# One step by seven products fewer in every second early block, and another order of the opening work

## The chip, the cores and the metric

The kernel runs on one core of one Trainium2 chip. Its time is device time in microseconds (us). Three runs of the kernel before took 1721.94, 1722.01 and 1723.89; the median is 1722.01. All times below are in us unless marked ns.

A core has a matrix engine (TensorE; PE in the profile, with its weight loads as PEld), an elementwise engine (VectorE; DVE), an engine for activation functions and copies with scale (ScalarE; ACT), GpSimd (POOL) and a queue engine (SyncE; SP) that here only starts transfers. Each engine works through its own instructions in the order in which they were written, and waits for the others by semaphores.

## What is computed

The reference is one layer of a decoder on 256 positions of width 2048, all in float32. Cut to what matters here:

```python
a = rmsnorm(h, norm_mix_pre)
proj = a @ w_in                        # 256 x 2048 times 2048 x 17408
q_a, k_a, v_a, q_r, f_r, i_r, g_r, gate_a, gate_r = split_columns(proj)
# three groups of sliding-window attention with rotary q and k
qh, kh = rotary(heads(q_a)), rotary(heads(k_a))
# a gated linear recurrence; its lower bound comes from hgrn_lower_bounds
f = lb + (1.0 - lb) * sigmoid(f_r)
r_out = norm(recurrence(silu(q_r), log(f), 1 - f, i_r)) * hgrn_norm_gain * silu(g_r)
y = sigmoid(gate_a) * (attn @ w_attn_branch) + sigmoid(gate_r) * (r_out @ w_hgrn_branch)
h = h + rmsnorm(y @ w_mix_out, norm_mix_post)
a = rmsnorm(h, norm_ffn_pre)
h = h + rmsnorm((silu(a @ W_gate) * (a @ W_up)) @ w_ffn_down, norm_ffn_post)
```

Here `lb` is the first entry of a softmax over the two rows of `hgrn_lower_bounds`. The first norm's factor per row is not multiplied into `a`; it is called `r1c` and is applied where the products leave the accumulators.

## The kernel before

Each float32 factor is split into a high and a low part (`hi` by a copy on ScalarE, `lo` by a subtraction on VectorE), and each product is made from three matmuls: high by high, high by low, low by high. The weights stream through SBUF: SP loads a `raw` tile, the two engines split it, TensorE multiplies.

**Blocks and steps.** The whole program is one list of steps, `seq` (main loop from L1351 on). A block is a set of output columns; a step is the part of a block with one slice of the contracted rows. In turn n the loop first issues the split of step n + 2 and the load for the unit three behind that one (`ahead`, `load_behind`), then the matmuls of step n, and then it advances some Python generators by one `yield` each: the evacuation of the block before (`evacs`), and two lanes of side work (`lanes[0]`, `lanes[1]`). So a `yield` in such a generator moves what follows it one step later, on every engine. The order on each engine is the order of this loop.

The list begins with two blocks for the gate `g_r` (halves 0 and 1, 8 steps each, 12 matmuls of 512 columns a step; steps 0 to 15). Then come the eight early blocks of the kind `Wide` (steps 16 to 79), each 1024 columns by 8 steps: four branch gates, three times the values `v`, and `i`. Behind them come the blocks with rotary, the recurrence, attention, the output projections and the feed-forward part.

**Steps by seven products.** In a `Wide` block a step covers two row groups (one pair `m`) and two column groups, so it is a 2 x 2 by 2 x 2 block product. A plain step makes it from eight products (24 matmuls of 512 columns). A step marked 1 in the block's order makes it from seven (21 matmuls), in the manner of Strassen and Winograd: `split_wide` (L319 to L349) first forms sums of weight quarters (`sum`, L333, L339, L340), splits these into `hi` (L338, L341) and `lo` (`wl`, L346), and splits three of the quarters themselves into `dh` (ScalarE, L344) and `dl` (VectorE, L348). A plain step needs one `hi` (L327) and one `lo` (`wl`, L329). On the other side a step by seven needs sums of the activations of its pair, `x7[m]`, which `pair_sums` (L415) makes in lane 1: a first part on VectorE (`f`, `s`; L420, L405 to L409), one copy on ScalarE (`so`, L411), one subtraction on VectorE (`so`, L413), each a step apart. The first nine of the 21 matmuls read `dh` and `dl`; the last twelve do not.

Two orders are used in the early blocks: `EIGHT` has steps by seven at the indices 2, 4 and 6 (pairs 0, 1, 2), `FOUR` at 1, 3, 5 and 6 (pairs 0, 1, 2, 3). Blocks 0, 2, 4 and 6 take `EIGHT`, blocks 1, 3, 5 and 7 take `FOUR`. The odd blocks exchange the roles of the two pools of accumulator banks (`flip`). Of `hi` there are three slots in turn, of `wl` three, of `sum` one, of `dh` and `dl` two each in the early blocks and one each in the feed-forward blocks, whose order is `EIGHT` too. When the last step by seven of a block is done, `gather` (L389) takes its four partial sums out of the banks, and the block's evacuation follows behind the last step.

**The opening.** `opening` (L580) runs in lane 0 from step 0: sums of squares, four transfers on ScalarE's queue (among them `rowg`, the rows with the norm gain and the lower bounds, and `cs`, cosines and sines); at step 8 the norm's factor `r1c`; then `row_broadcast` (L512), which writes `diag` on VectorE, multiplies it with ones on TensorE one step later and copies the result to `rowb` on ScalarE another step later; then the rotary tables `tabs` (L597); then a transpose of `rowg` on TensorE (L604), and from that the bounds `lb` and `lb1` (L606 to L617) with two Exp on ScalarE.

**The gate halves.** `evac_g` (L737) waits until `r1c` is announced in `ready`, then issues four activations from the accumulators (Sigmoid and Copy, L744, L745), yields once, and then issues per side two products on VectorE (L748, L749) and a store on POOL's queue, a side a step. For half 1 this runs during block 0. In a `Wide` block the evacuations still open are finished at once when the step with index `turn` is done; `turn` is 1 in the early blocks.

Of the kernel before, what the change touches and what calls it, by code (L numbers as in the profile page):

```python
# [14 lines left out]
F32R = mybir.dt.float32r  # L15
I32 = mybir.dt.int32
AF = mybir.ActivationFunctionType
OP = mybir.AluOpType
# [10 lines left out]
QSCALE = HD ** -0.5  # L29
# [3 lines left out]
COL_QR, COL_FR, COL_IR, COL_GR = 9216, 10240, 11264, 12288  # L33
COL_GA, COL_GB = 13312, 15360

X7, H7 = (0, 1, 2, 3), (0, 1, 2)
FOUR = [(4, 0), (0, 1), (5, 0), (1, 1), (6, 0), (2, 1), (3, 1), (7, 0)]
EIGHT = [(3, 0), (4, 0), (0, 1), (5, 0), (1, 1), (6, 0), (2, 1), (7, 0)]
DOWN = [[(m, m in by7) for m in range(KF // 2)] for by7 in (range(4, 20, 3), range(3, 19, 3))]

N_RAW, N_SPLIT, AHEAD, WARM, BRIDGE = 3, 3, 2, 8, 6


class Block:
# [46 lines left out]
def tile_hybrid_block(ctx: ExitStack, tc: tile.TileContext, t, out):  # L91
    nc = tc.nc
# [13 lines left out]
    def nm(s):  # L106
        serial[0] += 1
        return f"{s}_{serial[0]}"
# [7 lines left out]
    def aux():  # L116
        return auxp.tile([P, 512], F32, tag="aux", name=nm("aux"))
# [4 lines left out]
    def p3(s, dtype, n, bufs, tag=None):  # L122
        return pool["now"].tile([P, n], dtype, tag=tag or s, bufs=bufs, name=nm(s))
# [4 lines left out]
    def small(s, n=8, bufs=6):  # L128
        return cpool.tile([P, n], F32, tag=f"small{n}", bufs=bufs, name=nm(s))

    def mm(ps, lhsT, rhs, start, stop):
        nc.tensor.matmul(ps, lhsT, rhs, start=start, stop=stop, skip_group_check=True)  # L132
# [35 lines left out]
    r1c = cpool.tile([P, 2], F32, name="r1c")  # L168
# [3 lines left out]
    rowb = cpool.tile([P, S], F32, name="rowb")  # L172

    stage = ctx.enter_context(ExitStack())
    pool = {}
# [23 lines left out]
    cs = kp.tile([P, 2, S], F32, name="cs")  # L199
    gainr = kp.tile([P, HW], F32, name="gainr")  # L200
    tabs = kp.tile([P, 4, S], F32, name="tabs")
# [16 lines left out]
    def add_seven(*args, flip, **kw):  # L218
        b = Wide(*args, **kw)
        b.flip = flip  # L220
        blocks.append(b)
        for i in range(b.steps):
            seq.append(Step(b, i, len(units), 0))
            units.append([seq[-1]])
# [53 lines left out]
    def wslot():  # L278
        return stream.tile([P, 2048], F32R, tag="w", bufs=N_SPLIT, name=nm("w"))
# [39 lines left out]
    def split_wide(st):  # L319

        b, raw = st.block, st.raw
        m, by7 = b.order[st.i]
        prep = b.prep(m, by7) if b.prep else iter(())
        next(prep, None)
        hi, lo = wslot(), p3("wl", F32R, 2048, 3)
        if not by7:
            nc.scalar.activation(hi, raw, AF.Copy)  # L327
            next(prep, None)
            nc.vector.tensor_sub(lo, raw, hi.bitcast(F32))  # L329
            st.parts = hi, lo  # L330
            return
        s, d = p3("sum", F32, 2048, 1), raw[:, 512:]
        nc.vector.tensor_sub(  # L333
            s[:, :1024].rearrange("p (a c) -> p a c", a=2),
            raw[:, 512:1536].rearrange("p (a c) -> p a c", a=2),
            raw[:, None, :512].to_broadcast([P, 2, 512]),
        )
        nc.scalar.activation(hi[:, :1024], s[:, :1024], AF.Copy)  # L338
        nc.vector.tensor_add(s[:, 1024:1536], raw[:, 512:1024], s[:, 512:1024])  # L339
        nc.vector.tensor_sub(s[:, 1536:], raw[:, 1536:], s[:, 1024:1536])  # L340
        nc.scalar.activation(hi[:, 1024:], s[:, 1024:], AF.Copy)  # L341
        next(prep, None)
        dhi, dlo = (p3(x, F32R, 1536, 2 if pool["name"] == "early" else 1) for x in ("dh", "dl"))
        nc.scalar.activation(dhi, d, AF.Copy)  # L344
        for x in (slice(0, 2048),) if b.prep else (slice(0, 1024), slice(1024, 2048)):
            nc.vector.tensor_sub(lo[:, x], s[:, x], hi[:, x].bitcast(F32))  # L346
        next(prep, None)
        nc.vector.tensor_sub(dlo, d, dhi.bitcast(F32))  # L348
        st.parts = hi, lo, dhi, dlo  # L349
# [162 lines left out]
    def row_broadcast(dst, rc):  # L512

        ds = [small("diag", P, 2) for _ in range(2)]
        for b in range(2):
            nc.vector.tensor_scalar(ds[b], ident, rc[:, b : b + 1], None, op0=OP.mult)
        yield
        ps = aux()
        for b in range(2):
            mm(ps[:, b * P : (b + 1) * P], ones[:, :P], ds[b], True, True)  # L520
        yield
        nc.scalar.activation(dst, ps[:, :S], AF.Copy)
# [13 lines left out]
    ready = set()  # L536
# [24 lines left out]
    xT = Split("xT", KD)  # L561
# [18 lines left out]
    def opening():  # L580
        ss, s2 = small("ss"), small("s2")
        yield from sumsq(ss, xt[:3])
        nc.scalar.dma_start(gainr, t["hgrn_norm_gain"].to_broadcast([P, HW]))
        nc.scalar.dma_start(rowg[0:16], t["norm_ffn_pre"][0].rearrange("(a p) -> a p", p=P))
        nc.scalar.dma_start(
            rowg[16:32], t["hgrn_lower_bounds"].rearrange("l (a p) -> (l a) p", p=P)
        )
        nc.scalar.dma_start(cs, t["rope"])
        yield from sumsq(ss, xt[3:], 3)
        add_parts(s2[:, :2], ss)  # L590
        rsqrt_mean(r1c, s2[:, :2], D)
        ready.add("r1c")
        yield from row_broadcast(rowb, r1c)
        ready.add("rowb")
        yield
        for i, (j, c) in enumerate(((0, -QSCALE), (1, -QSCALE), (0, 1.0), (1, 1.0))):
            nc.vector.scalar_tensor_tensor(  # L597
                out=tabs[:, i, :].rearrange("p (two j) -> p two j", two=2),
                in0=cs[:, j, :].rearrange("p (j two) -> p two j", two=2), scalar=c,
                in1=rowb.rearrange("p (two j) -> p two j", two=2), op0=OP.mult, op1=OP.mult,  # L600
            )
        yield
        ps = aux()
        nc.tensor.transpose(ps[:, :32], rowg[:32], ident[:32, :32])  # L604
        yield
        nc.vector.tensor_copy(colg[:, 16:48], ps[:, :32])  # L606
        l0, l1 = colg[:, 32:40], colg[:, 40:48]
        m, e0, e1 = small("m"), small("e0"), small("e1")
        nc.vector.tensor_max(m, l0, l1)
        nc.vector.tensor_sub(e0, l0, m)  # L610
        nc.vector.tensor_sub(e1, l1, m)
        nc.scalar.activation(e0, e0, AF.Exp)
        nc.scalar.activation(e1, e1, AF.Exp)
        nc.vector.tensor_add(e1, e0, e1)
        nc.vector.reciprocal(e1, e1)
        nc.vector.tensor_mul(lb, e0, e1)
        nc.vector.tensor_scalar(lb1, lb, -1.0, 1.0, op0=OP.mult, op1=OP.add)  # L617
        ready.add("lb")

    def keep_warm(n):  # L620

        ps = aux()
        for _ in range(n):
            mm(ps, warm[:, :P], warm, True, True)
# [15 lines left out]
    x7 = {}  # L640
# [20 lines left out]
    def evac_kept(key, fn):  # L661
        def go(b):
            dst, at = keep(key, 1024), [(0, 0), (0, 1), (1, 0), (1, 1)]
            for k in at:
                nc.vector.tensor_add(b.rest[k], b.bank[k], b.rest[k])
            for s, g in at:
                e = b.rest[s, g]
                nc.scalar.activation(e, e, fn, scale=r1c[:, s : s + 1])
                nc.gpsimd.dma_start(dst[:, s, g * 512 : (g + 1) * 512], e)
                if (s, g) == (0, 1):  # L670
                    yield
            yield
        return go
# [63 lines left out]
    def evac_g(half):  # L737
        def go(banks):
            while "r1c" not in ready:
                yield  # L740
            dst, there = hslot("g"), keep(("g", half), 512)
            s = [ptile("sig") for _ in banks]
            for i, ps in enumerate(banks):
                nc.scalar.activation(s[i], ps, AF.Sigmoid, scale=r1c[:, i : i + 1])  # L744
                nc.scalar.activation(dst[:, i, :], ps, AF.Copy, scale=r1c[:, i : i + 1])  # L745
            yield
            for i in range(2):
                nc.vector.tensor_mul(dst[:, i, :], dst[:, i, :], s[i])  # L748
                nc.vector.tensor_mul(  # L749
                    dst[:, i, :], dst[:, i, :], gainr[:, half * 512 : (half + 1) * 512]  # L750
                )
                nc.gpsimd.dma_start(there[:, i, :], dst[:, i, :])
                yield
        return go
# [519 lines left out]
    w_in = t["w_in"][0]  # L1274
# [14 lines left out]
    for half in range(2):  # L1289
# [3 lines left out]
    early = [(COL_GA, ("a", 0), AF.Sigmoid), (COL_GB, ("r", 0), AF.Sigmoid),  # L1293
             (COL_GA + 1024, ("a", 1), AF.Sigmoid), (COL_GB + 1024, ("r", 1), AF.Sigmoid)]
    early += [(COL_V + 1024 * g, ("v", g), AF.Copy) for g in range(3)] + [(COL_IR, "i", AF.Copy)]
    for n, (col, key, fn) in enumerate(early):
        add_seven(w_in, (col, col + 512), FOUR if n % 2 else EIGHT, xT, lambda m: x7[m],
                  evac_kept(key, fn), flip=n % 2 == 1, turn=1,
                  pre=({0: lambda: advance(evacs), 1: lambda: flush(lanes[1])}).get(n))
    for half in range(2):  # L1300
        add_wide(w_in, KD, COL_FR + 512 * half, xT, evac_f(half))
# [49 lines left out]
    for n, st in enumerate(seq):  # L1351
        b, i = st.block, st.i
# [32 lines left out]
    a, b, c = seq[-3:]  # L1385
# [61 lines left out]
```

## Time and profile before

| what | value |
|---|---|
| median of three runs | 1722.01 |
| the profiled execution's own time | 1722.4 |
| its span in the trace | 1720.6 |
| granted TensorE clock, mean | 0.998 |
| TensorE (PE) busy | 1699.2 (99%) |
| VectorE (DVE) busy | 1404.6 (82%) |
| ScalarE (ACT) busy | 908.2 (53%) |
| read from HBM | 331.83 MB, 200 GB/s over the span |

A row of the timeline has the start in us from the begin of the span, the duration, engine, line, operation, the tiles written and read, the shapes and how many instructions the row merges; in square brackets stands the idle time of the engine before the row, and who ended it. A row of waits has who waited for whom, the sum in us, how often, and the longest. A row of windows has the stretch and its length, then busy time and instructions of each engine, the granted clock, the share of the DMA engines and GB/s. Durations of matmuls include their latency, and they overlap: the distance between two starts is what one costs. Some matmul records are missing from the trace, so counts of matmuls in a window can be a few too low.

### The profile page before, as it was taken

How to read it: one execution, taken by the hardware profiler on the slowest of the kernel's cores; microseconds unless marked ns; L12 is line 12 of the kernel's file. 1: busy time of each engine (PE TensorE's matmuls, PEld its weight loads, DVE VectorE, ACT ScalarE, POOL GpSimd, SP SyncE). 2: the span in 40 equal slices, each digit the busy share in tenths (PEclk: the TensorE clock that was granted, in tenths of full speed). 3: DMA queues.
4: the chain of work that ended last, by engine and by line, in shares of the span. 5: the costliest groups of instructions: out<-in, count | busy, mean ns of one | idle time of the engine just before them, and what ended most of it. 6: DMA issues, size and time to landing. Idle time of an engine off the chain costs nothing.

```text
span 1720.6 us, 21632 instructions
## 1 busy us (share of the span) xinstructions
PE 1699.2 (99%) x8334; PEld 1425.1 (83%) x8335; DVE 1404.6 (82%) x1577; ACT 908.2 (53%) x1027; POOL 40.1 (2%) x72
## 2 busy tenths in 40 slices
PE   9999999999999999999999999999999999999997
PEld 7788888878888898888888878888888888888886
DVE  6999898986677887877665578888888888898998
ACT  7556465554434434544444466555555555665663
POOL 0000000001000000000000000000000000000000
PEclk9999999999999999999999999999999999999999
DMA  8666666668544655465555745555555555666653
GB/s 279 212 216 242 211 229 219 230 211 285 173 166 164 214 163 174 160 207 172 171 171 183 258 161 206 196 199 201 202 202 201 202 201 198 207 198 216 200 197 117
DMA packets 206615, 344.79 MB, mean 200 GB/s; under 512 B 10960, under 2 KB 77568, under 8 KB 206512
## 3 DMA queue, kind: packets, MB, share of 16 engines
q1 hardware_dynamic: 198208, 317.89, 54.9%
q0 software_dynamic: 5680, 19.60, 3.3%
q10 hardware_dynamic: 2624, 5.92, 1.0%
q8 instruction: 65, 1.06, 0.2%
q14 instruction: 38, 0.31, 0.0%
HBM read 331.83 MB, written 11.53 MB: 200 GB/s over the span
## 4 chain that ended last, share of the span: by engine, by line
PE 77%; DVE 1%; ACT 1%; issue 1%; ACTq 0%; DVEq 0%
PE acc L132 52%; PE aux L132 23%; PE aux L818 0%; PE acc L1132 0%; DVE fz L1261 0%; PE aux L1132 0%; DVE dl L348 0%; PE aux L480 0%; PE aux L492 0%; ACT junk L1215 0%; ACT dh L344 0%; ACTq L1016 0%; DVE e L1211 0%; DVE sum L333 0%; ACT w L292 0%
## 5 line engine op out<-in xcount | busy, mean ns | idle before, releaser
L293 DVE TENSOR_TENSOR w<-raw,w 128x1024 fp32r<-128x1024 f32 (+1 forms) x225 | 274.1, 1219 | 189.0 <-ACT w L292 188.3
L292 ACT ACTIVATE w<-raw 128x1024 fp32r<-128x1024 f32 (+1 forms) x225 | 237.1, 1054 | 291.0 <-PE acc L132 243.1
L132 PE MATMUL acc<-xT,w 128*128 128x256 f32 (+1 forms) x2048 | 370.4, 339 | 0.0
L132 PEld LDWEIGHTS acc<-xT,w 128*128 128x128 f32 x2048 | 311.6, 188 | 43.3
L329 DVE TENSOR_TENSOR wl<-raw,w 128x2048 fp32r<-128x2048 f32 x118 | 269.9, 2289 | 76.1 <-ACT w L327 74.9
L327 ACT ACTIVATE w<-raw 128x2048 fp32r<-128x2048 f32 x118 | 225.0, 1909 | 112.0 <-PE aux L132 49.6
L132 PE MATMUL acc<-w,hT 128*128 128x512 f32 x622 | 181.5, 391 | 0.3 <-ACT hT L499 0.3
L338 ACT ACTIVATE w<-sum 128x1024 fp32r<-128x1024 f32 x70 | 74.4, 1063 | 190.2 <-DVE sum L333 181.1
L346 DVE TENSOR_TENSOR wl<-sum,w 128x1024 fp32r<-128x1024 f32 (+1 forms) x128 | 168.6, 1321 | 0.0
L132 PE MATMUL acc<-w,xT 128*128 128x512 f32 x480 | 139.3, 393 | 0.3 <-DVE w L293 0.2
L132 PEld LDWEIGHTS acc<-w,hT 128*128 128x128 f32 x622 | 116.0, 188 | 24.6 <-ACT hT L499 0.5
L132 PE MATMUL aux<-w,hT 128*128 128x512 f32 x430 | 135.6, 389 | 0.0
L348 DVE TENSOR_TENSOR dl<-raw,dh 128x1536 fp32r<-128x1536 f32 x70 | 123.0, 1757 | 8.8 <-ACT dh L344 6.7
L132 PE MATMUL aux<-w,xT 128*128 128x512 f32 x344 | 108.5, 389 | 0.0
L132 PEld LDWEIGHTS acc<-w,xT 128*128 128x128 f32 x480 | 89.2, 188 | 20.0 <-DVE w L293 1.6
L344 ACT ACTIVATE dh<-raw 128x1536 fp32r<-128x1536 f32 x70 | 103.1, 1473 | 0.0
L132 PEld LDWEIGHTS aux<-w,hT 128*128 128x128 f32 x430 | 80.7, 188 | 16.7
L132 PE MATMUL acc<-w,yT 128*128 128x512 f32 x384 | 88.2, 390 | 0.3 <-DVE w L293 0.3
L341 ACT ACTIVATE w<-sum 128x1024 fp32r<-128x1024 f32 x70 | 74.4, 1062 | 21.5 <-DVE sum L340 21.5
L333 DVE TENSOR_TENSOR sum<-raw 128x1024 f32<-128x1024 f32 x70 | 85.2, 1217 | 0.2 <-DMA raw<-in_w_ffn_down 0.2
L132 PEld LDWEIGHTS acc<-w,yT 128*128 128x128 f32 x384 | 71.8, 188 | 15.5 <-DVE w L293 0.7
L132 PE MATMUL aux<-w,a 128*128 128x512 f32 x268 | 83.7, 389 | 0.0
(261 smaller groups left out, 2737.8 us busy)
## 6 DMA issues: line engine op xcount, KB each, us to landing
raw<-in_w_in SPq DMA_DIRECT2D x271, 512.0 KB, 4.5
raw<-in_w_ffn_gate_up SPq DMA_DIRECT2D x176, 512.0 KB, 4.4
raw<-in_w_ffn_down SPq DMA_DIRECT2D x88, 512.0 KB, 4.8
raw<-in_w_mix_out SPq DMA_DIRECT2D x32, 512.0 KB, 4.9
kept<-e POOLq DMA_DIRECT2D x32, 256.0 KB, 4.4
raw<-in_w_hgrn_branch SPq DMA_DIRECT2D x16, 512.0 KB, 4.9
raw<-in_w_attn_branch SPq DMA_DIRECT2D x16, 512.0 KB, 4.5
v<-kept POOLq DMA_DIRECT2D x8, 512.0 KB, 7.3
```

Source lines behind the costliest of these rows:

```text
L132: nc.tensor.matmul(ps, lhsT, rhs, start=start, stop=stop, skip_group_check=True)
L292: nc.scalar.activation(wh[:, k], raw[:, k], AF.Copy)
L293: nc.vector.tensor_sub(wl[:, k], raw[:, k], wh[:, k].bitcast(F32))
L327: nc.scalar.activation(hi, raw, AF.Copy)
L329: nc.vector.tensor_sub(lo, raw, hi.bitcast(F32))
L333: nc.vector.tensor_sub(s[:, :1024].rearrange("p (a c) -> p a c", a=2), raw[:, 512:1536].rearrange("p (a c) -> p a c", a=2), raw[:, None, : ...
L338: nc.scalar.activation(hi[:, :1024], s[:, :1024], AF.Copy)
L341: nc.scalar.activation(hi[:, 1024:], s[:, 1024:], AF.Copy)
L344: nc.scalar.activation(dhi, d, AF.Copy)
L346: nc.vector.tensor_sub(lo[:, x], s[:, x], hi[:, x].bitcast(F32))
L348: nc.vector.tensor_sub(dlo, d, dhi.bitcast(F32))
```

## The change

All eight early blocks take the order `EIGHT`: three steps by seven, of the pairs 0, 1 and 2. The order `FOUR` and the sums of the fourth pair, `x7[3]`, are gone; `more_x` still starts the pairs 0 and 2 at step 6 and now pair 1 alone at step 7. `dh` and `dl` have one buffer each in all stages.

In `opening` the transpose of `rowg` comes directly behind the norm's factor, in the same step; the bounds follow in the next two steps; `r1c` is announced after the two Exp, one step later than before; then comes `row_broadcast`; and the rotary tables come after 16 more yields, which is in step 28, in block 1. The announcement of `rowb`, which nothing waited for, is gone.

For half 1 of the gate, `evac_g` yields four times instead of once between its activations and its products, and block 0 finishes open evacuations only at its step with index 6 instead of 1.

```diff
-X7, H7 = (0, 1, 2, 3), (0, 1, 2)
-FOUR = [(4, 0), (0, 1), (5, 0), (1, 1), (6, 0), (2, 1), (3, 1), (7, 0)]
+X7 = H7 = (0, 1, 2)
 EIGHT = [(3, 0), (4, 0), (0, 1), (5, 0), (1, 1), (6, 0), (2, 1), (7, 0)]
...
-N_RAW, N_SPLIT, AHEAD, WARM, BRIDGE = 3, 3, 2, 8, 6
+N_RAW, N_SPLIT, AHEAD, WARM, BRIDGE, LATER = 3, 3, 2, 8, 6, 16
...
-        dhi, dlo = (p3(x, F32R, 1536, 2 if pool["name"] == "early" else 1) for x in ("dh", "dl"))
+        dhi, dlo = (p3(x, F32R, 1536, 1) for x in ("dh", "dl"))
...
         rsqrt_mean(r1c, s2[:, :2], D)
-        ready.add("r1c")
-        yield from row_broadcast(rowb, r1c)
-        ready.add("rowb")
-        yield
-        for i, (j, c) in enumerate(((0, -QSCALE), (1, -QSCALE), (0, 1.0), (1, 1.0))):
-            nc.vector.scalar_tensor_tensor(
-                out=tabs[:, i, :].rearrange("p (two j) -> p two j", two=2),
-                in0=cs[:, j, :].rearrange("p (j two) -> p two j", two=2), scalar=c,
-                in1=rowb.rearrange("p (two j) -> p two j", two=2), op0=OP.mult, op1=OP.mult,
-            )
-        yield
         ps = aux()
         nc.tensor.transpose(ps[:, :32], rowg[:32], ident[:32, :32])
         yield
...
         nc.scalar.activation(e0, e0, AF.Exp)
         nc.scalar.activation(e1, e1, AF.Exp)
+        ready.add("r1c")
+        yield
         nc.vector.tensor_add(e1, e0, e1)
         nc.vector.reciprocal(e1, e1)
         nc.vector.tensor_mul(lb, e0, e1)
         nc.vector.tensor_scalar(lb1, lb, -1.0, 1.0, op0=OP.mult, op1=OP.add)
         ready.add("lb")
+        yield from row_broadcast(rowb, r1c)
+        for _ in range(LATER):
+            yield
+        for i, (j, c) in enumerate(((0, -QSCALE), (1, -QSCALE), (0, 1.0), (1, 1.0))):
+            nc.vector.scalar_tensor_tensor(
+                out=tabs[:, i, :].rearrange("p (two j) -> p two j", two=2),
+                in0=cs[:, j, :].rearrange("p (j two) -> p two j", two=2), scalar=c,
+                in1=rowb.rearrange("p (two j) -> p two j", two=2), op0=OP.mult, op1=OP.mult,
+            )
...
-            yield
+            for _ in range(1 if half == 0 else 4):
+                yield
             for i in range(2):
                 nc.vector.tensor_mul(dst[:, i, :], dst[:, i, :], s[i])
...
-        add_seven(w_in, (col, col + 512), FOUR if n % 2 else EIGHT, xT, lambda m: x7[m],
-                  evac_kept(key, fn), flip=n % 2 == 1, turn=1,
+        add_seven(w_in, (col, col + 512), EIGHT, xT, lambda m: x7[m],
+                  evac_kept(key, fn), flip=n % 2 == 1, turn=1 if n else 6,
```

## The prediction

> **What bounds the kernel now.** I read the page's busy shares first, then busy time stage by stage, then what PE waited for, then the timelines of the places where it waited. The page:
>
> ```profile
> span 1720.6 us, 21632 instructions
> ...
> PE 1699.2 (99%) x8334; PEld 1425.1 (83%) x8335; DVE 1404.6 (82%) x1577; ACT 908.2 (53%) x1027; POOL 40.1 (2%) x72
> ```
>
> TensorE is the bound; a change can gain only by fewer matmuls or by filling PE's gaps. The early blocks, one window per block (us; PE, PEld, DVE, ACT and POOL busy with counts; granted clock, DMA share, GB/s):
>
> ```profile
> 56.10:101.14 45.04, 42.34 (x184) 34.20 (x183) 43.26 (x43) 25.67 (x23) 1.08 (x2) 1.00 0.63 223
> 101.14:144.25 43.11, 41.41 (x182) 33.65 (x181) 40.61 (x36) 24.99 (x22) 2.17 (x4) 1.00 0.63 219
> 144.25:185.72 41.47, 41.47 (x185) 34.35 (x184) 36.23 (x33) 22.35 (x20) 2.16 (x4) 1.00 0.66 229
> 185.72:228.81 43.09, 41.42 (x182) 33.64 (x181) 40.60 (x36) 24.96 (x22) 2.17 (x4) 1.00 0.63 220
> ...
> 270.28:313.35 43.07, 41.40 (x182) 33.63 (x180) 40.58 (x36) 24.95 (x22) 2.17 (x4) 1.00 0.64 219
> 313.35:354.83 41.48, 41.48 (x185) 34.35 (x183) 36.25 (x33) 22.36 (x20) 2.16 (x4) 1.00 0.68 229
> 354.83:397.86 43.03, 41.38 (x181) 33.63 (x180) 39.66 (x37) 24.93 (x24) 3.11 (x6) 1.00 0.62 208
> ```
>
> Blocks 2 and 6 (and 4, left out) have three steps by seven products and PE is busy in the whole window. Blocks 1, 3, 5 and 7 have four, so 12 matmuls less than eight plain steps instead of 9, and yet they take longer, with PE idle for 1.7. Block 0 has three and takes 45.04. PE's waits between 40 and 400 us, and the longest one behind that:
>
> ```profile
> PE acc L132 <- DVE dl L348: 6.7, 8, 0.9
> PE aux L132 <- DVE dl L348: 1.3, 1, 1.3
> PE aux L132 <- DVE wl L329: 0.9, 1, 0.9
> PE aux L132 <- ACT dh L344: 0.5, 1, 0.5
> ```
>
> ```profile
> PE aux L492 <- DVE h L1065: 0.8, 1, 0.8
> ```
>
> Eight waits for dl are two in each four-step block; the other three rows are block 0. On PE's timeline:
>
> ```profile
> 57.42 0.50 PE L132 MATMUL aux<-wl,xT 128*128 128x512 f32 x1 [0.93 <-DVE wl L329]
> ...
> 68.21 0.39 PE L132 MATMUL aux<-dh,xT 128*128 128x512 f32 x1
> ...
> 72.06 0.39 PE L132 MATMUL acc<-w,so 128*128 128x512 f32 x1
> ...
> 79.05 0.50 PE L132 MATMUL aux<-dh,xT 128*128 128x512 f32 x1 [0.47 <-ACT dh L344]
> 80.84 0.50 PE L132 MATMUL aux<-dl,xT 128*128 128x512 f32 x1 [1.29 <-DVE dl L348]
> ```
>
> From 68.21 to 72.06 PE issues the first to the 18th matmul of one step: 3.85/17 = 0.2265 a matmul. So a plain step (24) takes 5.44 and one by seven (21) 4.76. The 0.39 of a row is its latency, not its price.
>
> Why VectorE is late in a four-step block: here is VectorE where its split of a step by seven begins (sum), and where a plain step's begins (wl, L329).
>
> ```profile
> 118.07 2.29 DVE L329 TENSOR_TENSOR wl<-raw,w 128x2048 fp32r<-128x2048 f32 x1
> 120.28 1.22 DVE L333 TENSOR_TENSOR sum<-raw 128x1024 f32<-128x1024 f32 x1
> ...
> 127.13 1.22 DVE L333 TENSOR_TENSOR sum<-raw 128x1024 f32<-128x1024 f32 x1
> ```
>
> A plain step costs VectorE 2.2 (118.07 to 120.28), one by seven 6.85 (120.28 to 127.13). A plain one and one by seven are 9.1 against 10.2 on PE: VectorE keeps up. Two by seven in a row, as indices 5 and 6 of the four-step order are, are 13.7 against 9.5: it falls behind. That is the second wait; the first, at index 3, comes since index 1's split lies just before the evacuation of the block before.
>
> **The change part by part.** *Three steps everywhere.* Blocks 1, 3, 5 and 7 become what 2, 4 and 6 are, with only the roles of the bank pools exchanged. I take the measured difference: 43.11, 43.09, 43.07 and 43.03 against 41.47 and 41.48 is 1.64 + 1.62 + 1.60 + 1.56 = 6.4 less. It contains 3 x 0.2265 = 0.68 for the added matmuls of each block, 2.7 in all; the vanished waits, with the restart behind each, are the other 9.1. Each converted step gives VectorE 6.85 - 2.2 = 4.6 back. [...]
>
> *One dh and one dl instead of two.* ScalarE's dh of a step may now start only when PE is through with the dh of the one by seven before. In block 2:
>
> ```profile
> 167.13 0.39 PE L132 MATMUL acc<-dh,xT 128*128 128x512 f32 x1
> ...
> 169.14 1.48 ACT L344 ACTIVATE dh<-raw 128x1536 fp32r<-128x1536 f32 x1
> ```
>
> PE's last use of the old dh ends at 167.52; the next dh, with a second buffer at hand, was written only from 169.14. The reason is structural: hi of that split comes earlier on ScalarE and needs the w slot that PE frees just before it begins the step whose dh is in question. So the added wait has ended 1.6 earlier: nothing. If that cover went, ScalarE would stand with the next hi queued behind dh.
>
> *The opening.* I number steps from 0: 0-7 and 8-15 are the two gate halves, 16-23 block 0. Rows between the norm and step 16:
>
> ```profile
> 37.36 0.16 DVE L150 SCALAR_TENSOR_TENSOR r1c<-a,y 128x2 f32<-128x2 f32 x1
> ...
> 37.90 1.28 ACT L744 ACT_TABLE_LOAD   x1
> ...
> 41.49 1.07 ACT L292 ACTIVATE w<-raw 128x1024 fp32r<-128x1024 f32 x1
> ...
> 43.74 0.69 DVE L748 TENSOR_TENSOR g<-g,sig 128x512 f32<-128x512 f32 x1
> ...
> 45.07 1.22 DVE L293 TENSOR_TENSOR w<-raw,w 128x1024 fp32r<-128x1024 f32 x1
> ...
> 47.53 1.42 DVE L597 SCALAR_TENSOR_TENSOR tabs<-cs,rowb 128x256 f32<-128x256 f32 x4
> ...
> 51.75 0.18 DVE L606 COPY colg<-aux 128x32 f32<-128x32 f32 x1
> ...
> 53.43 0.68 DVE L420 TENSOR_TENSOR f<-xT 128x512 f32<-128x512 f32 x1
> ...
> 55.09 2.28 DVE L329 TENSOR_TENSOR wl<-raw,w 128x2048 fp32r<-128x2048 f32 x1
> ```
>
> PE's first wait is for the wl that starts at 55.09 and ends at 57.37; VectorE has no long gap from 45.07 (split of step 13) to there, 12.3. Between those points the change takes away the tables (1.4) and the bounds (51.75 to 53.43, 1.7) and puts in the first pair of gate products, which comes one step later as r1c is announced one step later (43.74 to 45.07, 1.3): 10.5. But the stretch also begins later. ScalarE's two Exp now come first, behind VectorE's so, one split and four small bounds operations (37.5 + about 2.4 = 39.9); Exp to 40.2, split of 12 to 41.2, then table load and four gate evacuations (37.90 to 41.49: 3.6), so, and the split of 13 to about 46.4. Queued behind the Exp on ScalarE are those splits; PE takes up step 12 only at about 44.4 (the row of 48 matmuls below begins with step 6; 27.77 + 72 x 0.2265, and a transpose between), so that wait is hidden. 46.4 + 10.5 = 56.9 against 57.37: of the wait at 57.42 only about 0.45 goes. The ends: nothing of it goes, or all of it (0.93 by its row, some 1.2 with the restart). Two table loads of 1.28 leave ScalarE, off the path.
>
> Two new orders on PE: the transpose of rowg moves to the end of step 8, the matmuls with ones to the end of step 11. The first waits for a DMA:
>
> ```profile
> 27.77 11.14 PE L132 MATMUL acc<-w,xT 128*128 128x512 f32 x48
> ```
>
> ```profile
> L585 ACTq DMA_DIRECT2D rowg<-in_hgrn_lower_bounds x1: 442/442/442, 29.0 to 29.0; - x1
> ```
>
> ```profile
> rowg<-in_hgrn_lower_bounds ACTq DMA_DIRECT2D x1, 8.0 KB, 6.1
> ```
>
> It lands at 35.1; step 8 ends at 27.77 + 36 x 0.2265 = 35.9. Nothing, with 0.8 to spare. The ones need diag: behind the sums of an x pair (1.66 from 39.9), the split of 12, the rest of the bounds and diag itself, some 2.4 together, that is 44.0; PE is there at 44.4. The tables go to step 28, behind the split of a step by seven, where the even blocks' VectorE is idle for some us (41.47 - 36.23 = 5.2 a block): nothing.
>
> *Block 0's second wait*, at step 20 (79.05 and 80.84). Ahead of that split on VectorE lay:
>
> ```profile
> 67.33 0.69 DVE L748 TENSOR_TENSOR g<-g,sig 128x512 f32<-128x512 f32 x1
> ...
> 68.66 0.69 DVE L420 TENSOR_TENSOR f<-xT 128x512 f32<-128x512 f32 x1
> ...
> 72.52 0.68 DVE L748 TENSOR_TENSOR g<-g,sig 128x512 f32<-128x512 f32 x1
> ...
> 73.85 1.22 DVE L333 TENSOR_TENSOR sum<-raw 128x1024 f32<-128x1024 f32 x1
> ```
>
> The gate products (1.33 twice) now come behind the splits of 21 and 22, and the sums of the fourth x pair (68.66 on, 1.66) are gone: 4.3 less, with 0.45 from above, so dl stands at about 80.8 - 4.75 = 76.0. PE wants it at 78.6 - 0.45 = 78.1. The wait goes. Next at risk is dl of step 22: one product pair (1.33) is back before it, so it comes 3.4 earlier, while PE comes 2.7 earlier; there was no wait, and there is none. The gate's stores on POOL move some steps; nothing stands behind them until block 0's stores. SP's loads follow the splits that free their raw, which are earlier.
>
> Block 0: 45.04 - 41.47 = 3.57 above an undisturbed block; about 0.85 stays: 2.7 gained. **Sum: 6.4 + 2.7 = 9.1.** The profiled execution is 1722.4 (span 1720.6 and 1.8 around it), so 1713.3; it is 0.4 above the runs' median of 1722.01, so I forecast 1712.9 as a median. The block-0 term runs from 2.3 (its first wait stays whole) to 3.57 (both go), and I allow the 0.4 between profiled execution and median once downwards: 1711.6 to 1713.3.
>
> **The rivals.** *Block 0's loss stays* (its products only move to collide with step 22, or rowg is late): 1722.0 - 6.4 = 1715.6. For it: slack at 22 is thin. *One of the two waits of an odd block survives*, four times about 1.1: 1722.0 - 9.1 + 4.4 = 1717.3. Against: VectorE is less loaded than in front of block 2, which had no wait.
>
> *The gain is given back later*, because what follows goes by transfers and not by PE: about 1722. Against it: behind 400 us PE's longest wait is 0.8.
>
> *Slower: the single dh and dl.* If ScalarE, now ahead, meets dh's release late, hi of the next step stands behind it, and the second and third steps by seven of eight blocks (16) each cost a wait like those seen, 9.1/8, about 1.1: 1712.9 + 17.6 = 1730.5. It decides where ScalarE's dh would come more than 1.6 earlier, relative to PE, than in block 2. [...] The row speaks against: the repeating gap is ended by VectorE's dl.
>
> **How the numbers follow.** Forecast 0.60; block 0 keeps its loss 0.17; one wait per odd block survives 0.09; still better than 1711.6 by a cause I don't see 0.03; given back 0.06; slower 0.05. Forecast and the first rival hold 0.77, so the range takes in the second too: 1711.6 to 1717.4. A measurement here can tell about 0.2%, 3.4 us: faster 0.60 + 0.17 + 0.09 + 0.03 = 0.89, same 0.06, slower 0.05.
>
> **What would show it.** Odd blocks of 41.5 with PE busy throughout; no PE wait for dl after block 0; the first wl of block 0 late by under 1 us; tables in block 1 with no PE wait near; dh never ended by PE. Wrong if PE waits for ScalarE's dh, or if PE waits in steps 8 to 15.

## The result and the profile after

The changed kernel took 1712.80 us (median of four runs, 1712.62 to 1713.05), the kernel before 1721.97 beside it (four runs, 1721.72 to 1723.89): 9.2 less. The ratio is 0.9944, with a 95% interval from 0.9927 to 0.9962. The forecast was 1712.9. The profiled execution took 1712.74, 1.74 of it around its span. The page of the changed kernel, its lines on span and busy time:

```profile
span 1711.0 us, 21621 instructions
...
PE 1699.0 (99%) x8347; PEld 1428.4 (83%) x8347; DVE 1385.0 (81%) x1551; ACT 898.8 (53%) x1016; POOL 40.1 (2%) x72
```

PE's busy time is the same as before to 0.2, although twelve matmuls were added: a busy record lasts longer (0.39 by its row) than a matmul costs (0.2265 from start to start), and the records are not complete (8347 against 8334, 13 more for twelve matmuls), so this line can't show the change. VectorE has 19.6 less. The early blocks, one window per block as in the prediction (us; PE, PEld, DVE, ACT, POOL busy; granted clock, DMA share, GB/s):

```profile
55.61:98.00 42.39, 41.82 (x185) 34.29 (x184) 40.87 (x36) 23.92 (x21) 1.08 (x2) 1.00 0.72 248
98.00:139.47 41.47, 41.47 (x184) 34.37 (x183) 37.51 (x36) 22.95 (x20) 2.17 (x4) 1.00 0.68 231
139.47:180.96 41.49, 41.49 (x185) 34.37 (x184) 36.25 (x32) 22.93 (x20) 2.16 (x4) 1.00 0.66 228
180.96:222.43 41.47, 41.47 (x184) 34.36 (x183) 36.22 (x32) 22.90 (x20) 2.17 (x4) 1.00 0.66 228
...
346.88:388.35 41.47, 41.47 (x184) 34.37 (x183) 35.42 (x33) 22.86 (x22) 3.25 (x6) 1.00 0.64 216
```

Seven blocks now take 41.47 to 41.49 and PE is busy in the whole of each. The eight blocks together go from 341.76 to 332.74: 9.0. Block 0 begins 0.5 earlier. Most of that half is not the change's: `r1c`, which is computed from the same instructions in both kernels, stands at 36.97 here and at 37.36 before. Over all profiles of this study block 0 began between 55.26 and 56.43, without a relation to what was edited: the changed kernel itself stands at 55.61 here and at 55.94 in its second profile. PE's waits between 40 and 400 us, all of them:

```profile
PE aux L131 <- DVE wl L328: 0.6, 1, 0.6
```

One wait is left of eleven. (The lines of the changed file are one less than before in `split` and the matmul helper.)

### The profile page after: what moved, and what is told of

Same layout as the page of the kernel before. It is cut to its first block, busy times and chain, and to the rows that moved or that the text cites. A ratio compares the mean times of both kernels' runs of the same rounds, so it can differ in the third digit from the quotient of the medians.

```text
span 1711.0 us, 21621 instructions
## 1 busy us (share of the span) xinstructions
PE 1699.0 (99%) x8347; PEld 1428.4 (83%) x8347; DVE 1385.0 (81%) x1551; ACT 898.8 (53%) x1016; POOL 40.1 (2%) x72
## 4 chain that ended last, share of the span: by engine, by line
PE 97%; DVE 1%; DMA 1%; ACT 1%; issue 0%; SPq 0%; DVEq 0%; ACTq 0%
PE acc L131 63%; PE aux L131 32%; PE aux L818 0%; DMA gpost<-in_norm_mix_post 0%; DMA raw<-in_w_in 0%; PE aux L491 0%; PE acc L1132 0%; DVE fz L1261 0%; DVE w L292 0%; PE aux L1132 0%; PE aux L479 0%; ACT junk L1215 0%; DVE e L1211 0%; DVE wl L328 0%; ACT w L291 0%
## 5 line engine op out<-in xcount | busy, mean ns | idle before, releaser
L328 DVE TENSOR_TENSOR wl<-raw,w 128x2048 fp32r<-128x2048 f32 x122 | 279.3, 2289 | 83.9 <-ACT w L326 82.6
L326 ACT ACTIVATE w<-raw 128x2048 fp32r<-128x2048 f32 x122 | 233.1, 1910 | 133.8 <-PE aux L131 59.4
L345 DVE TENSOR_TENSOR wl<-sum,w 128x1024 fp32r<-128x1024 f32 (+1 forms) x120 | 159.0, 1328 | 0.0
L337 ACT ACTIVATE w<-sum 128x1024 fp32r<-128x1024 f32 x66 | 70.1, 1063 | 168.0 <-DVE sum L332 168.0
L131 PE MATMUL acc<-w,xT 128*128 128x512 f32 x536 | 156.0, 392 | 0.3 <-DVE w L292 0.2
L347 DVE TENSOR_TENSOR dl<-raw,dh 128x1536 fp32r<-128x1536 f32 x66 | 116.0, 1757 | 8.2 <-ACT dh L343 4.9
L131 PEld LDWEIGHTS acc<-w,xT 128*128 128x128 f32 x536 | 99.8, 188 | 22.1 <-DVE w L292 1.4
L343 ACT ACTIVATE dh<-raw 128x1536 fp32r<-128x1536 f32 x66 | 97.2, 1473 | 0.0
L131 PE MATMUL acc<-w,a 128*128 128x512 f32 x268 | 83.7, 389 | 0.0
L131 PE MATMUL acc<-wl,hT 128*128 128x512 f32 x215 | 83.7, 389 | 0.0
```

## The experiments

The kernels ran in sets of four, four and three, each set on one chip. The kernel before ran beside each set, with medians of 1722.57, 1722.41 and 1722.77; the ratios are to it.

**The order alone.** The kernel before, with these two lines changed:

```diff
-X7, H7 = (0, 1, 2, 3), (0, 1, 2)
+X7 = H7 = (0, 1, 2)
...
-        add_seven(w_in, (col, col + 512), FOUR if n % 2 else EIGHT, xT, lambda m: x7[m],
+        add_seven(w_in, (col, col + 512), EIGHT, xT, lambda m: x7[m],
```

> The kernel before with the three-step order in all eight early blocks and the sums of the fourth pair gone; opening, gate products and two dh/dl buffers as before. Theory (VectorE's queue sets PE's waits): odd blocks 41.5 us with no PE wait, 6.4 gained; in block 0 VectorE has 1.66 less ahead of the split of step 20, so that wait shrinks from 2.3 to about 0.6, the wait at step 16 stays at 1.1; block 0 about 43.4; time 1722.0 - 8.1 = 1713.9. Rival (the order makes the whole gain, the rest of the change is worth nothing): 1712.8. Rival (the other parts make half or more of it): above 1717.

Measured: 1714.26 (1713.92 to 1714.46), ratio 0.9951 (0.9939 to 0.9964). The windows of blocks 0 and 1, and PE's waits:

```profile
56.06:99.49 43.43, 42.09 (x184) 34.19 (x183) 41.25 (x36) 25.72 (x22) 1.08 (x2) 1.00 0.68 232
99.49:140.97 41.48, 41.48 (x184) 34.35 (x183) 36.26 (x32) 22.94 (x20) 2.17 (x4) 1.00 0.68 228
```

```profile
PE aux L132 <- DVE wl L329: 1.0, 1, 1.0
PE aux L132 <- DVE dl L348: 0.4, 1, 0.4
```

This is the theory's result in each place: block 1 is clear and no other odd block has a wait, block 0 is at 43.4, the wait at step 16 is whole, and that at step 20 has shrunk by about the sums that are gone. The order by itself is worth 8.3 of the 9.2.

**The opening alone.** The changed kernel with `FOUR`, the fourth pair and two buffers put back:

```diff
-        add_seven(w_in, (col, col + 512), EIGHT, xT, lambda m: x7[m],
+        add_seven(w_in, (col, col + 512), FOUR if n % 2 else EIGHT, xT, lambda m: x7[m],
```

> The changed kernel with the four-step order back in the odd blocks, its fourth pair of sums and two dh/dl buffers; opening and gate products as changed. Theory: the odd blocks keep their two waits and 43.1 us; block 0 loses the wait at step 20 and 0.45 of the one at step 16, about 42.3; the tables fall into block 1 behind its last split by seven and cost nothing; time 1722.0 - 2.7 = 1719.3. Rival (the products only move to collide with step 22): 1721 to 1722. Rival (the tables lengthen block 1's waits by their 1.4): 1720.7.

Measured: 1720.87 (1720.50 to 1721.66), ratio 0.9990 (0.9981 to 0.9999). The gain is less than the theory had it, and the time alone fits the rival with the tables (1720.7) and nearly the one with step 22 (from 1721). Windows of blocks 0, 1 and 2:

```profile
55.84:98.57 42.73, 42.11 (x184) 34.19 (x183) 41.39 (x41) 22.73 (x21) 1.08 (x2) 1.00 0.70 232
98.57:142.94 44.37, 41.73 (x182) 33.55 (x180) 41.88 (x40) 25.90 (x22) 2.17 (x4) 1.00 0.67 225
142.94:184.42 41.48, 41.48 (x185) 34.35 (x183) 37.45 (x35) 22.40 (x20) 2.16 (x4) 1.00 0.71 233
```

Block 0 gains 2.3, and block 1 is 1.26 longer than before. PE's rows in block 1 that VectorE ended:

```profile
109.93 0.50 PE L132 MATMUL acc<-wl,xT 128*128 128x512 f32 x1 [0.78 <-DVE wl L329]
116.79 0.50 PE L132 MATMUL acc<-dl,xT 128*128 128x512 f32 x1 [1.12 <-DVE dl L348]
```

There is a new wait at 109.93, for a plain step's wl, and the next one is longer. The tables are not the cause: they run at 132.69 on VectorE, behind both. Step 22 is a small part: its first dl matmul begins at 88.47, 0.52 behind the one before it, so 0.3 late, and that lies within block 0's 42.73. My expectation had added parts as if each stood alone. I formed another reason: in a block of four steps by seven VectorE has no slack, so what PE gains in front of it waits there for the same backlog. That is tested below.

**Two buffers.** The changed kernel, with one line put back:

```diff
-        dhi, dlo = (p3(x, F32R, 1536, 1) for x in ("dh", "dl"))
+        dhi, dlo = (p3(x, F32R, 1536, 2 if pool["name"] == "early" else 1) for x in ("dh", "dl"))
```

> The changed kernel with two buffers each for dh and dl in the early blocks. Theory: with one buffer nothing waits for its release, so there is no difference: 1712.8, all blocks within 0.05 us of the changed kernel's. Rival (one buffer holds ScalarE up, which the margins hide only partly): 1711.5 or less, block 0's step-16 wait or the margins in front of dl change by over 0.3.

Measured: 1712.35 (1712.27 to 1713.39), ratio 0.9942 (0.9930 to 0.9955). The windows of blocks 0 and 1 are those of the changed kernel to 0.03:

```profile
55.26:97.62 42.36, 41.79 (x185) 34.27 (x183) 40.86 (x36) 23.93 (x21) 1.08 (x2) 1.00 0.75 251
97.62:139.10 41.48, 41.48 (x185) 34.35 (x183) 37.51 (x36) 22.95 (x20) 2.17 (x4) 1.00 0.70 230
```

**One buffer in the old order.** The kernel before with one buffer, the place where it would hurt first:

> The kernel before with one buffer each for dh and dl in the early blocks and nothing else. Here two steps by seven stand next to each other, so this is where one buffer would hurt first. Theory (the repeating gap is VectorE's time, not the number of buffers): PE's last use of the old dh ends about when ScalarE gets to the next, 130.4 against 130.8 in block 1, so at most 0.1 a block: 1722.0 to 1722.4. [...]

Measured: 1722.57 (1721.80 to 1724.07) against 1722.41, ratio 1.0001 (0.9992 to 1.0010). PE's waits, the same four rows as before:

```profile
PE acc L132 <- DVE dl L348: 6.6, 8, 0.9
PE aux L132 <- DVE dl L348: 1.3, 1, 1.3
PE aux L132 <- DVE wl L329: 0.9, 1, 0.9
PE aux L132 <- ACT dh L344: 0.5, 1, 0.5
```

With these two runs the slower rival is gone. So is, for dh and dl, the reading that the repeating gap is a matter of the number of buffers: going from two buffers to one left the gap as it was (eight waits of 6.6 us together, 6.7 before). More than two, or more buffers for the other tiles of a split, no run tried in the old order, so a deeper lookahead stays an untested way to the same gain.

**Gate products early.** The changed kernel, with block 0 as before in this point:

```diff
-            for _ in range(1 if half == 0 else 4):
+            for _ in range(1):
                 yield
...
-                  evac_kept(key, fn), flip=n % 2 == 1, turn=1 if n else 6,
+                  evac_kept(key, fn), flip=n % 2 == 1, turn=1,
```

> The changed kernel with the second half's gate products one yield behind their activations and open evacuations of block 0 finished at its second step, as before. Theory: 2.66 of VectorE work is back ahead of the split of step 20, whose dl was ready 2.07 before PE asked: it is now late by about 0.6, with the restart 0.7; time 1713.5, block 0 about 43.1. Rival (the sums of the fourth pair alone were too much, and the later gate products change nothing): no wait at step 20, 1712.8.

Measured: 1713.72 (1712.95 to 1714.14), ratio 0.9948 (0.9935 to 0.9960). The time alone can't carry this half microsecond over the spread of runs; the rows can. Block 0, and PE's wait at step 20, which the changed kernel does not have:

```profile
56.40:99.34 42.94, 42.11 (x185) 34.19 (x183) 40.78 (x36) 23.83 (x21) 1.08 (x2) 1.00 0.73 248
```

```profile
79.03 0.50 PE L131 MATMUL aux<-dl,xT 128*128 128x512 f32 x1 [0.34 <-DVE dl L347]
```

Block 0 is 0.55 longer. So the later products are worth that much with three pairs of sums, and the rival is refuted.

**First half later.** The changed kernel, with the first half's products moved too, to clear the wait that is left:

```diff
-            for _ in range(1 if half == 0 else 4):
+            for _ in range(3 if half == 0 else 4):
```

> The changed kernel with the first gate half's products two yields later (three yields behind their activations instead of one), so that one pair of them (1.33) goes behind the split of step 16. Theory: VectorE alone makes the wait left at step 16 (0.73 more than a matmul's distance); it goes, block 0 from 42.4 to 41.6, time 1712.8 - 0.8 = 1712.0; the margin of dl in front of step 18 shrinks from 1.06 to about 0.2. Rival (the wait only moves to step 18): the same time, with a wait for dl at step 18.

Measured: 1712.50 (1711.75 to 1712.84), ratio 0.9941 (0.9927 to 0.9955). PE has no wait at all between 40 and 400 us, and block 0 is 0.91 shorter:

```profile
55.50:96.98 41.48, 41.48 (x184) 34.35 (x183) 40.42 (x36) 22.50 (x19) 1.64 (x3) 1.00 0.71 243
```

The medians differ by 0.3 where 0.8 was expected, and that the time is lower than the changed kernel's can't be told from these runs; that the wait was VectorE's, and that it does not move to step 18, can.

**Four with gaps.** The changed kernel with four steps by seven in the odd blocks, never two in a row, and the fourth pair of sums:

```diff
-X7 = H7 = (0, 1, 2)
+X7, H7 = (0, 1, 2, 3), (0, 1, 2)
+SPACED = [(0, 1), (4, 0), (1, 1), (5, 0), (2, 1), (6, 0), (3, 1), (7, 0)]
...
-        add_seven(w_in, (col, col + 512), EIGHT, xT, lambda m: x7[m],
+        add_seven(w_in, (col, col + 512), SPACED if n % 2 else EIGHT, xT, lambda m: x7[m],
```

> The changed kernel with four steps by seven again in the odd blocks, but at the indices 0, 2, 4 and 6 (never two in a row), and the fourth pair of sums; one buffer for dh and dl. Theory (VectorE is late only where two steps by seven follow each other or where the evacuation lies in between): odd blocks 40.8 us, 0.68 less each, margin at index 2 about 0.1; block 0 as changed, since the 1.66 of the fourth pair fit in the 2.07 of step 20; time 1712.8 - 2.7 = 1710.1. Rival (four steps by seven are too much for VectorE in any order, as a block then has 4 x 6.85 + 4 x 2.2 + 5.5 = 41.7 of its work): odd blocks at 41.7 or more, 1713 or more. Rival (one buffer is too few for four): PE or ScalarE waits around dh, 1715 or more.

Measured: 1717.57 (1717.22 to 1718.90), ratio 0.9971 (0.9959 to 0.9982): 7.5 over what I expected. Windows of blocks 1, 2 and 3, then PE and VectorE at the start of block 1:

```profile
98.46:145.48 47.02, 43.00 (x181) 34.68 (x180) 43.19 (x43) 23.70 (x21) 2.17 (x4) 0.96 0.67 224
145.48:186.95 41.47, 41.47 (x184) 34.35 (x183) 39.05 (x35) 24.27 (x21) 2.16 (x4) 1.00 0.68 226
186.95:227.95 41.00, 41.00 (x181) 33.70 (x180) 37.76 (x34) 23.03 (x20) 2.17 (x4) 1.00 0.68 233
```

```profile
104.28 0.52 PE L132 MATMUL aux<-dh,xT 128*128 128x512 f32 x1 [4.02 <-DVE e L665]
```

```profile
101.35 2.28 DVE L329 TENSOR_TENSOR wl<-raw,w 128x2048 fp32r<-128x2048 f32 x1
103.55 2.47 DVE L665 TENSOR_TENSOR e<-aux,e 128x512 f32<-128x512 f32 x4
```

Block 3 does what the theory said, 41.00 where 40.8 was expected, so four steps by seven are not too much when they have gaps. Block 1 is the failure. A step by seven at index 0 needs the banks of its partial sums at once, and in an odd block these are the banks in which the four outputs of the block before still stand. VectorE empties them at L665, and here it came to that late, with the gathering of block 0's partial sums (from 98.56) and the split at 101.35 in front. I had counted splits and had left out the banks. The rival with one buffer has its time (1715 or more), but not its wait: PE's waits in this run are for L665, wl and dl, none is for dh.

**Both.** The last two edits together:

> Both of the last two edits together. Theory: the gains add: 1712.8 - 0.8 - 2.7 = 1709.3, block 0 at 41.6 and odd blocks at 40.8. Rival (block 0's margins are used up by the first edit, so the fourth pair's sums make a wait at step 20): 0.3 to 1 less gain, 1709.6 to 1710.3.

Measured: 1717.40 (1717.00 to 1718.68), ratio 0.9972 (0.9961 to 0.9983). The same gap in block 1 (4.0 us by the waits) hides whether the two gains add.

**Four from block 3 on, in the old order.** The changed kernel with `FOUR if n in (3, 5, 7) else EIGHT` and the fourth pair, to test the reason formed above:

> The changed kernel with the old four-step order in blocks 3, 5 and 7 only, and the fourth pair's sums in block 0 as before. It asks where the run with the new opening and the old orders lost 1.3 us of block 0's gain, in block 1. Theory (a block of four steps by seven is bound by VectorE, so what PE gains in front of it waits there for the same backlog; a block of three has the slack to take it up): block 1 41.5 with no wait, blocks 3, 5 and 7 43.1, time 1712.8 + 3 x 1.6 + 0.35 for block 0's small wait at step 22 = 1718.0. Rival (the tables or the late gate products make the loss, whatever order block 1 has): block 1 at 42.7 or more, 1719.2 or more.

Measured: 1718.06 (1717.72 to 1718.77), ratio 0.9973 (0.9963 to 0.9983). Windows of blocks 0 to 3:

```profile
56.43:99.23 42.80, 42.07 (x184) 34.19 (x183) 41.49 (x40) 24.34 (x21) 1.08 (x2) 1.00 0.71 240
99.23:140.71 41.48, 41.48 (x184) 34.36 (x183) 38.80 (x38) 23.03 (x20) 2.17 (x4) 1.00 0.71 237
140.71:182.19 41.48, 41.48 (x184) 34.36 (x183) 36.18 (x33) 22.29 (x20) 2.16 (x4) 1.00 0.69 228
182.19:225.26 43.07, 41.40 (x181) 33.64 (x180) 40.59 (x36) 24.94 (x22) 2.17 (x4) 1.00 0.65 219
```

Block 0 is as in the run with the opening alone, the tables and the late products are there, and block 1 with three steps by seven takes 41.48 and gives nothing back. So the loss needs block 1's order. How that order makes it is read from the run with the opening alone, from VectorE's and ScalarE's rows in front of the new wait at 109.93:

```profile
103.69 2.47 DVE L665 TENSOR_TENSOR e<-aux,e 128x512 f32<-128x512 f32 x4
107.59 2.29 DVE L329 TENSOR_TENSOR wl<-raw,w 128x2048 fp32r<-128x2048 f32 x1 [1.42 <-ACT w L327]
```

```profile
104.41 1.34 ACT L668 ACTIVATE e<-e,r1c 128x512 f32<-128x512 f32 x2 [2.43 <-DVE e L665]
105.66 1.90 ACT L327 ACTIVATE w<-raw 128x2048 fp32r<-128x2048 f32 x1
```

VectorE has no idle time from 86.65 to 106.16, so there is a backlog. But then it stands idle for 1.42, until ScalarE has made the `hi` (L327) of the next plain step. ScalarE has that behind the first evacuation activations (L668), and these had waited 2.43 for VectorE's L665. So it is a chain through both engines, and not VectorE's lack of time alone; the kernel before has the same 1.42 at 108.88, in front of its first wait in block 1. In block 1 of the run shown here, with three steps by seven, VectorE has a like idle time (1.27 at 110.32), and PE does not come to wait for it. No run cut this chain by itself.

**Four with gaps from block 3 on.** The first half's products later, `SPACED if n in (3, 5, 7) else EIGHT`, and the fourth pair's sums made in block 1:

```diff
-                  pre=({0: lambda: advance(evacs), 1: lambda: flush(lanes[1])}).get(n))
+                  pre=({0: lambda: advance(evacs),
+                        1: lambda: (flush(lanes[1]), lanes[1].append(pair_sums(xT, (3,), x7, lambda: rslot("so")))),
+                        3: lambda: flush(lanes[1])}).get(n))
```

> The changed kernel with the first gate half's products two yields later, block 1 kept at three steps by seven, and blocks 3, 5 and 7 with four at the indices 0, 2, 4 and 6; the fourth pair's sums are made during block 1. Theory (the four-step order with gaps failed only in block 1, where block 0's outputs still stood in the banks): no long wait anywhere, blocks 0, 1 and the even ones 41.5, blocks 3, 5 and 7 41.0, time 3 x 0.47 = 1.4 under the kernel with the later products, 2.0 to 2.3 under the changed kernel. Rival (the banks collide in front of each block that begins with a step by seven): a gap of 4 us and a lower clock in three blocks, 10 us or more above the changed kernel.

**The changed kernel again**, beside it on the same chip:

> The changed kernel itself, on the same chip as the other two: 1712.8, block 0 at 42.4 and all others at 41.5.

Measured: 1710.71 (1710.42 to 1711.12) for the first, ratio 0.9932 to the kernel before (0.9920 to 0.9945), and 1712.98 (1712.49 to 1713.66) for the changed kernel, ratio 0.9946 (0.9933 to 0.9958). The five runs of each don't overlap: 2.3 less, as expected. Blocks 0, 1 and 3 of the faster one:

```profile
55.89:97.37 41.48, 41.48 (x184) 34.36 (x183) 40.41 (x36) 22.52 (x19) 1.64 (x3) 1.00 0.72 243
97.37:138.85 41.48, 41.48 (x184) 34.36 (x183) 39.76 (x43) 23.66 (x21) 2.18 (x4) 1.00 0.69 234
...
180.34:221.37 41.03, 41.03 (x181) 33.71 (x180) 37.76 (x34) 23.02 (x20) 2.18 (x4) 1.00 0.68 233
```

PE has no wait between 40 and 400 us here. This version beats both kernels. By the rows the banks are free only just in time, though: in block 3 the first of VectorE's four additions at L665 runs from 181.03 to 181.7, and PE's first matmul into such a bank begins here:

```profile
181.76 0.50 PE L132 MATMUL aux<-dh,xT 128*128 128x512 f32 x1
```

It starts 0.30 behind the matmul before it, the next one 0.34 behind it, instead of 0.2265. This is most of what block 3 is longer than the 40.8 that was first expected.

## Why the prediction was right, point by point

**Three steps everywhere: 6.4 forecast.** Blocks 1, 3, 5 and 7 went from 43.11, 43.09, 43.07 and 43.03 to 41.47 each: 6.42. The run with the order alone shows that no other part is needed for it. The sum took the measured difference of the windows, so it did not hang on the reason given for the two waits. That reason was VectorE's time alone; for the first of them the rows have ScalarE's evacuation in the chain as well (under **Four from block 3 on, in the old order**).

**One dh and dl: nothing.** The two runs on buffers show it from both sides, and between 56 and 400 us ScalarE never waits for PE to write dh. In block 2 of the changed kernel dh is written from 164.31; PE's last use of the one before began at 162.37 and lasts 0.39, so 1.55 lie between, where the prediction had 1.6:

```profile
162.37 0.39 PE L131 MATMUL acc<-dh,xT 128*128 128x512 f32 x1
```

```profile
164.31 1.47 ACT L343 ACTIVATE dh<-raw 128x1536 fp32r<-128x1536 f32 x1
```

**The opening: 0.45 forecast, the rest of the wait stays.** VectorE's rows in the changed kernel:

```profile
36.97 0.16 DVE L149 SCALAR_TENSOR_TENSOR r1c<-a,y 128x2 f32<-128x2 f32 x1
...
45.90 1.23 DVE L292 TENSOR_TENSOR w<-raw,w 128x1024 fp32r<-128x1024 f32 x1 [2.55 <-ACT w L291]
...
54.23 2.29 DVE L328 TENSOR_TENSOR wl<-raw,w 128x2048 fp32r<-128x2048 f32 x1
```

The stretch from the split of step 13 to the end of wl is 45.90 to 56.52: 10.6, forecast 10.5. In front of it VectorE stands idle for 2.55, since ScalarE has the table load (1.28) and the gate evacuations ahead of that split (40.68 to 44.79), as the prediction worked out. PE's own wait went from 0.93 to 0.57, and PE waits nowhere in steps 8 to 15. From r1c to the end of wl it is 19.55 against 20.01 before: 0.46 less. Here the reading of two queues gave a better number than the plain thought that work moved away is time won: the stretch became 1.7 shorter (12.3 to 10.6), and it began 1.2 later, counted from r1c.

**Step 20: the wait goes.** VectorE's dl, and when PE took it:

```profile
73.99 1.76 DVE L347 TENSOR_TENSOR dl<-raw,dh 128x1536 fp32r<-128x1536 f32 x1
```

```profile
77.82 0.39 PE L131 MATMUL aux<-dl,xT 128*128 128x512 f32 x1
```

It is ready 2.07 early; the prediction had 76.0 against 78.1. The parts: without the fourth pair's sums the wait is 0.4 (the order alone); the later gate products take the rest away (the run that puts them back). They clear step 20 with the fourth pair's sums in place too: in the run with the opening alone dl is ready at 77.43 and PE takes it at 77.98. Step 22, the place I called thin, has a margin of 1.76 in the changed kernel. With the later gate products it does fail in each run that keeps the fourth pair's sums in block 0: there the first dl matmul comes 0.3 later than the usual distance in three runs, and 0.6 later where the first half's products come late as well. The margin stands on these sums, and on more of them than the prediction counted: beside the 1.66 in front of step 20's split, they have a subtraction (`so`, L413) of 0.60 behind it, at 80.70 in the kernel before, which the working for step 22 left out. That error was to the safe side.

**Tables and rowg: nothing.** The tables run at 126.04 in block 1, with no wait of PE near. `rowg` landed at 28.6 + 6.1 = 34.7, PE's transpose of it ran at 35.8.

**The sum: 9.1 forecast, 9.2 measured.** The windows of the eight blocks bear it out with 9.0. That the median came within 0.1 of the forecast is partly luck: the changed kernel's own medians were 1712.80 and 1712.98, and those of the kernel before lie between 1721.97 and 1722.77. Block 0 kept 42.39 - 41.47 = 0.92 of its loss, forecast 0.85. What was not right is the picture that the parts add: by the windows the opening alone gives less than half of its block-0 gain in the end, since block 1 in the old order takes 1.26 of 2.31 back. In the sum this did not show, because the change makes block 1 a block of three.

## What to carry to other kernels

A trick that saves the bounding engine some work (21 matmuls instead of 24) has to be priced on the engine that prepares it too: here each saved 0.68 of TensorE cost VectorE 4.6, and two in a row turned the saving into a wait. Where neighbouring pieces of a program already run in both forms, their two window lengths forecast a conversion; here they were right to 0.1 in 6.4. Then ask what is taken back behind it: a gain in front of a stretch that the helping engines fill can be lost there again, and a form that needs all its banks in its first step can collide with the evacuation of the piece before: in block 1 it cost a wait of 4.0, in block 3 about 0.2.

## What the runs showed of the hardware

In the run of four with gaps PE stood for 4.0 us at the start of block 1, and that cost more than the gap. Windows of that kernel around it (us; the clock granted stands behind the five engines), and two of PE's rows behind the gap:

```profile
99.90:104.20 4.30, 0.36 (x2) 0.00 (x0) 4.20 (x6) 0.00 (x0) 0.00 (x0) 1.00 0.69 237
104.20:105.00 0.80, 0.72 (x2) 0.60 (x3) 0.80 (x3) 0.74 (x2) 0.00 (x0) 0.77 0.52 61
105.00:108.40 3.40, 3.40 (x10) 2.65 (x9) 3.33 (x5) 1.66 (x2) 1.08 (x2) 0.55 0.97 352
108.40:111.80 3.40, 3.40 (x17) 2.77 (x16) 3.25 (x4) 3.16 (x4) 0.00 (x0) 1.00 0.27 101
```

```profile
105.03 0.63 PE L132 MATMUL aux<-dh,xT 128*128 128x512 f32 x1
105.45 0.63 PE L132 MATMUL aux<-w,so 128*128 128x512 f32 x1
```

Over the 3.4 us from 105.0 the granted clock was 0.55 on average (0.77 in the 0.8 before), and matmuls came 0.42 apart instead of 0.2265; the eight from 105.03 to 108.26 took 3.2 instead of 1.8. Up to 104.20, through the wait itself, the clock stood at 1.00, and it was at 1.00 again in the 3.4 us from 108.4. The other waits of this study, up to 1.29 us idle by their rows, left the clock at 1.00 in every window shown. The kernel before shows a fall of the clock too, where PE has nothing more to do: its last matmul begins at 1711.53 and lasts 0.39.

```profile
1713.00:1714.00 1.00, 0.00 (x0) 0.00 (x0) 0.64 (x2) 0.94 (x4) 0.00 (x0) 1.00 0.00 0
1714.00:1715.00 1.00, 0.00 (x0) 0.00 (x0) 0.84 (x4) 0.05 (x1) 0.00 (x0) 0.69 0.00 0
1715.00:1716.00 1.00, 0.00 (x0) 0.00 (x0) 1.00 (x3) 0.00 (x0) 0.00 (x0) 0.50 0.21 61
```

There the clock was still at 1.00 when PE had stood for 2.1 us, and at 0.50 after 3.1; in the run of four with gaps it was at 1.00 for the first 3.9 us of the wait. So the runs don't show one length of idle time after which it falls, and between 40 and 400 us none of them has a wait of PE between 1.29 and 4.0 us.

Block 1 with that wait took 47.02, block 3 in the same order 41.00: 6.0 more for 4.0 us of waiting, 1.5 for each. In the kernel before, the eight waits for dl, 6.7 us together, cost 9.1 (6.4 by the windows and 2.7 for the twelve matmuls), 1.36 for each. So here one wait of 4 us was dearer than four of 1 us would be at that rate, an estimated 5.4, which I had not put into the sum for this run.
